# Two weight sums of attention's values formed in DRAM, a bias loaded around its masked corner, and squares ahead of low parts

## The chip, the core and the metric

One core of one Trainium2 chip runs the kernel. The metric is device time of one execution in microseconds (us). The kernel before takes 2188.28 us, the median of 3 runs (2187.18 to 2188.38). The execution that the profiler recorded is a further one and took 2192.47 us; the span from its first to its last instruction is 2190.8 us.

A core has one TensorE (PE; its weight loads are shown as PEld), one VectorE (DVE), one ScalarE (ACT), one GpSimd (POOL) and SyncE (SP), which here only issues transfers. 16 DMA engines carry the transfers of all queues. [...]

## What is computed

One layer of an encoder for 512 tokens of width 2048, all in 32-bit floats. `h = RMSNorm(x)` is multiplied by one input projection, whose columns give two head groups. Group A is attention with 16 heads of 64, over the own chunk of 64 tokens and the 8 chunks before it, with a learned bias by relative distance. Group B is gated linear attention with 4 heads. Both results go through `w_out` and are added to x. A gated MLP with a causal convolution of width 3 follows (two up-projections of 5632 columns, one down-projection), then a gate by a per-layer embedding, and a last RMSNorm.

```python
s = einsum('bqhd,bkhd->bhqk', qc, kb) * scale + bias      # attention, one chunk of queries
s = where(valid, s, neg); pr = softmax(s); y = einsum('bhqk,bkhd->bqhd', pr, vb)
x = x + concat(y_a, y_g) @ w_out
u = causal_depthwise_conv(rms_norm(x) @ w_ffn_up); x = x + (gelu(u_gate) * u_val) @ w_ffn_down
x = x + sigmoid(rms_norm(x) @ w_ple_gate) * (p @ w_ple_proj);  out = rms_norm(x)
```

With 512 tokens, 8 chunks of 64 and a band of 9 chunks, attention is causal by chunks: a query sees all keys of its own chunk and of those before it. Two chunks of queries share one tile of 128 rows, so in the last 128 keys of a tile the first 64 rows must not see the last 64 keys. That 64 x 64 corner is the masked corner of the bias tile.

## The kernel before

**Products with seven multiplications.** The large matrix products are done by a Strassen-like scheme: weights and activations are split into 2 x 2 blocks, and seven products P1, P2, P6, P5, P7, P3, P4 of block sums give the four blocks of the result (`PRODUCTS`). The weight operands are L11, L12, L22 (blocks as they are) and the sums S1 = L21+L22, S2 = S1+L11, S4 = S2+L12, S3 = L21+L11. Each 32-bit operand is further split in two parts, a high part (ACT copies the page to a reduced type) and a low part (DVE subtracts the high part from the page), and each product is three matmuls: high x high, high x low, low x high. So every weight page of 128 x 1024 costs one ACT copy, one DVE subtraction, and then matmuls on PE. The high/low pages of weights live in a ring of three.

**The stages in order.** (1) `first_values` and `second_values`: the values of group B, a plain product over 16 blocks of the contraction, in two halves of 512 columns; 8 weight pages each, with 24 matmuls of 512 columns a page. In the same time the root mean square of x, the gates and the pieces and block differences of the normed x are formed. (2) The values of attention by seven products (`VALUE_ORDER`: P1, P2, P4, P5, P6, P3, P7), four weight pages each, numbered n = 0 to 27, with 12 matmuls of 512 columns a page. (3) The front stage: 16 units of the input projection, each seven products of 24 matmuls of 256 columns. The first four units feed the linear attention, the next eight the attention (`attend`), the last four the output gates. (4) `wo`, the up-projection, three slices of the down-projection, the embedding gate, the end.

**Order of the work.** In the values' stages the order on ACT, DVE, PE, SP and POOL is the order in which the code is written (`in_order(True, True)`, L1423); in the later stages the loads may move. A wait of one instruction holds up all that stands behind it on its engine. `keep_in_program_order` puts one instruction behind what was written before it for its engine.

**The value pages of attention.** `values_product` (L1205) does for page n, in this order: load page n+4 if it is among the first 12, split page n+2 (`value_split`: ACT's high part, DVE's low part), do what the plan at L1581 lists for n, then PE's 12 matmuls. P1, P2 and P4 use L11, L12 and L22, loaded by SP into a ring of four pages. For S1, S2, S4, one page a block j stays in SBUF (`sum_load` L1182 loads L21 at n = 1, 3, 5, 7) and grows: for j = 0, 1 POOL accumulates L22 onto it (`sum_more` at n = 4 and 6), for j = 2, 3 DVE adds the L22 page, kept from P4 (`sum_right` L1192 at n = 10 and 11). After P5's split POOL accumulates L11 (n = 11 to 14, pages of P6), after P6's split L12 (n = 15 to 18, pages of P3). For P7, SP loads L21 into the ring at n = 7, 8, 11, 12, and POOL accumulates L11 at n = 8, 9, 19, 20.

**Attention's bias.** One tile of 128 x 2 x 512 holds the bias of the two heads of a unit. Unit 0's is loaded by `first_bias` (L1621), each later one by `load_e` (L813), 2 transfers of 256 KB, after the unit before has read the tile last. Then `mask` (L817) has DVE write the corner with -1e30, four steps after the unit's products, and two steps later `soft(0)` (L855) reads the bias first.

**A step.** In the front stage and later each step is one product of one unit: items of rank 0 (transfers), the high part of step i+2 (`prep_high`), items of rank 1, the low part of step i+2 (`prep_low`, L1646), the product, items of rank 2 to 8, the collection of the product.

**Squares.** In the stages `wo` and the last slice of the down-projection, `squares` (L627) adds the squares of the result to `acc`, ACT squaring and DVE adding; PE's sum over `acc` (tile `ms`) stands after the twelfth product of the next stage (`norm_step`, L1146), and its place on PE is fixed.

Of the kernel before, what the change touches and what calls it, by code (L numbers as in the profile page):

```python
# [12 lines left out]
ALU = mybir.AluOpType  # L13

P = 128
T = 512
# [26 lines left out]
def encoder_block(ctx: ExitStack, tc: tile.TileContext, A, out):  # L43
# [210 lines left out]
    def first_values(src, second):  # L254
        ps = [psum_mm(f"v0_{t}") for t in range(TT)]
        for kp in range(KD // 2):
            if kp == 4:
                gate_weights()
            xs = []
            if kp > 0:  # L260
                xs.append(load_input(2 * kp))
            hi, lo = wtile(src[0, kp], f"wv0_{kp}", 2 if kp < 2 else 1,
                           (lambda: xs.append(load_input(0))) if kp == 0 else None)
            xs.append(load_input(2 * kp + 1))
            sq_acc(xs[0], kp == 0)
            sq_acc(xs[1], False)
            if kp == KD // 2 - 1:
                in_order(True)
                first_stats()
            values_page(ps, hi, lo, kp)  # L270
        next(second)
        values_out(ps, 0, [gt(f"t{t}") for t in range(TT)])
# [354 lines left out]
    def squares(unit, at, c=slice(0, T)):  # L627

        def square(s):
            if unit.first and s == 0:  # L630
                act.activation(acc[:, c], unit.xs[:, s, c], AF.Square)
            else:
                sqt[unit, s] = tp.tile([P, T], F32, tag=("sq", "dg")[s], name="sq")[:, c]
                act.activation(sqt[unit, s], unit.xs[:, s, c], AF.Square)

        def add(s):
            if (unit, s) in sqt:
                vec.tensor_tensor(acc[:, c], acc[:, c], sqt[unit, s], ALU.add)

        return [(at + i, k, lambda f=f, s=s: f(s)) for i, k, f, s in ((0, 2, square, 0), (1, 2, square, 1), (1, 2, add, 0),  # L640
                                                                      (2, 2, add, 1))]

    sqt = {}

# [154 lines left out]
        move(3)  # L799


    TILES = ((3,), (2,), (1, 0))
    att, bias = [], []
    ypair = []

    def attend(unit):
# [4 lines left out]
            return att[0].tile([P, cols], dt, tag=tag or name, name=name, bufs=bufs)  # L811

        def load_e():  # L813
            for s in range(2):
                nc.sync.dma_start(bias[0][:, s, :], A["bias"][2 * b + s])

        def mask():  # L817
            vec.memset(bias[0][0:64, :, T - CHUNK:T], NEG)

        def load_v():  # L820
            M["V"] = tile_("va", T).rearrange("p (k v) -> p k v", k=TT)
# [364 lines left out]
    def sum_more(v, n, name):  # L1186
        prod, j = v["pages"][n]
        raw = v["raw"][n] if prod == "P7" else v["sum"][j]
        v["raw"][n] = raw
        pool.dma_start(raw, value_page(name, j), accum_op=ALU.add)  # L1190

    def sum_right(v, j):  # L1192
        vec.tensor_tensor(v["sum"][j], v["sum"][j], v["l22"].pop(j), ALU.add)
        v["raw"][12 + j] = v["sum"][j]

    def value_split(v, n):
        if n < len(v["pages"]):
            raw = v["raw"].pop(n)
            if v["pages"][n][0] == "P4":
                v["l22"][v["pages"][n][1]] = raw  # L1200
# [187 lines left out]
    def second_values(src):  # L1388
        raw, tiles = {}, {}
        first = {"ps": None}  # L1390

        def load(k):
            if k < KD // 2:
                raw[k] = page("wr", f"wv1_{k}_r")
                syn.dma_start(raw[k], src[1, k])
            else:
                if k == KD // 2:
                    use_rings({"wr": ("r1", "r2", "r0", "r3")})
                value_load(va, k - KD // 2)
# [9 lines left out]
        todo = {0: [(gate_low,), (scale_pair, 2), (right, 0)],  # L1409
                1: [(scale_pair, 3), (differences, 0), (right, 1)],  # L1410
                2: [(gate_up,), (gate_abs, (0, 1)), (scale_pair, 4), (gate_min, (0, 1))],
                3: [(gate_abs, (2, 3)), (scale_pair, 5), (gate_min, (2, 3)), (right, 2)],
                4: [(gate_exp, (0, 1, 2, 3)), (scale_pair, 6), (differences, 1), (right, 3)],
                5: [(gate_ln, (0, 1, 2, 3)), (scale_pair, 7), (differences, 2)],
                6: [(spread_differences, 0), (differences, 3), (spread_differences, 1)],
                7: [(spread_differences, 2), (spread_differences, 3), (right, 4), (differences, 4)]}
        for k in range(3):
            load(k)
        split_page(0)
        split_page(1)  # L1420
        load(3)
        yield
        in_order(True, True)  # L1423
        scale_pair(0)
        scale_pair(1)
        ps = [psum_mm(f"v1_{t}") for t in range(TT)]
        for k in range(KD // 2):
            load(k + 4)
            split_page(k + 2)
# [132 lines left out]
        nc.gpsimd.memset(G["attn"], 0.0)  # L1562
        G["s"] = pg.tile([P, 2, T], F32R, tag="r6", name="squares")

    va = dict(pages=[(p, j) for p in VALUE_ORDER for j in range(4)], raw={}, sum={}, l22={}, tiles={}, have=set())

    def at_page(n, *fs):
        plan.setdefault(n, []).extend(fs)
# [11 lines left out]

    for n, *fs in ((0, (second_out, (0, 1)), (spread_differences, 4)),  # L1581
                   (1, (second_out, (2, 3)), (sum_load, va, 0), (right, 5), (right, 6)), (2, (differences, 5)),
                   (3, (sum_load, va, 1), (spread_differences, 5)), (4, (right, 7), (sum_more, va, 12, "L22")),
                   (5, (sum_load, va, 2), (differences, 6)), (6, (sum_more, va, 13, "L22"), (spread_differences, 6)),
                   (7, (sum_load, va, 3), (differences, 7)), (9, (spread_differences, 7)),
                   (12, (gate_sum, (0, 1))), (13, (gate_scan, (0,))), (14, (gate_sum, (2, 3))), (15, (gate_scan, (1,))),
                   (16, (gate_scan, (2,))), (17, (gate_scan, (3,))),
                   (10, (sum_right, va, 2)), (11, (sum_right, va, 3)),
                   *((i, (value_load, va, 24 + j)) for j, i in enumerate((7, 8, 11, 12))),
                   *((11 + j, (sum_more, va, 16 + j, "L11")) for j in range(4)),  # L1590
                   *((15 + j, (sum_more, va, 20 + j, "L12")) for j in range(4)),
                   *((i, (sum_more, va, 24 + j, "L11")) for j, i in enumerate((8, 9, 19, 20))),
                   *((18 + i, (gate_decay, (i,))) for i in range(4)),
                   *((22 + i, (gate_small, (i,))) for i in range(4)), (26, (linear_pages,)),
                   *((n, (give, tag)) for n, tag in ((19, "r4"), (20, "r5"), (23, "r1"), (24, "r2"), (25, "r0"), (26, "r3")))):
        at_page(n, *(lambda f=f, a=a: f(*a) for f, *a in fs))
# [308 lines left out]
```

## Time and profile before

| what | us |
|---|---|
| median of 3 runs | 2188.28 |
| the profiled execution | 2192.47 |
| its span | 2190.8 |
| PE busy in the span | 2174.8 (99%) |
| DVE busy | 1862.3 (85%) |
| ACT busy | 1332.1 (61%) |
| POOL busy | 215.0 (10%) |

A row of the timeline gives the start, the duration of a run of like instructions, engine, line, operation, the tile written and the tiles read, shapes, their number, and in brackets the engine's idle time before it with what ended it. Most instructions carry line 64, a helper's, so they are told apart by tiles: `v` are the matmuls of group B's values, `vaA` to `vaD` those of attention's values (vaA first P1, then P6, then P7; vaB P2; vaD P4; vaC P5, then P3), `accA` to `accC` those of the later units, `w` the high and low parts of weights, `wva_s` the growing sum pages, `wva_P_r` the ring pages, `psc` scores, `sc` the scores with bias, `ptr` transposed probabilities, `ms` the sum of squares. PE's rows overlap a little, since matmuls are pipelined; the pace is read from starts. SPq and POOL rows of DMA_DIRECT2D are issues; the transfer itself lands later.

### The profile page before, as it was taken

The numbers are of one execution on the slowest core, as the hardware profiler recorded it, in microseconds if no ns is written. First come the engines' busy times: TensorE is split into PE (matmuls) and PEld (weight loads), VectorE is DVE, ScalarE is ACT, GpSimd is POOL, SyncE is SP. The second block draws the span as 40 slices with busy tenths as digits, with TensorE's granted clock in tenths as the row PEclk, the third lists the DMA queues.
The fourth block names the chain that finished last, engine by engine and source line by source line (L and its number), as shares of the span: only waits on it lengthen the run. The fifth ranks groups of instructions, "written<-read, shape, count | busy, mean of one in ns | idle before, by whom it ended". The sixth has DMA issues, their size and how long they took to land.

```text
span 2190.8 us, 45672 instructions
## 1 busy us (share of the span) xinstructions
PE 2174.8 (99%) x18262; PEld 2126.2 (97%) x18262; DVE 1862.3 (85%) x2558; ACT 1332.1 (61%) x1976; POOL 215.0 (10%) x261
## 2 busy tenths in 40 slices
PE   9999999999999999999999999999999999999998
PEld 7879998999999999999999999999999999999998
DVE  6977878887788889999888888888898787898898
ACT  6654567777675665555555555555564554666766
POOL 0121011111000011111111100000000101000000
PEclk9999999999999999999999999999999999999999
DMA  5598888898978989999999987887875976979996
GB/s 193 168 262 228 221 242 228 227 245 239 373 266 261 362 234 278 290 298 300 290 278 290 271 240 215 228 221 202 261 249 159 302 221 179 325 253 353 292 286 223
DMA packets 198277, 561.65 MB, mean 256 GB/s; under 512 B 21968, under 2 KB 60112, under 8 KB 198064
## 3 DMA queue, kind: packets, MB, share of 16 engines
q1 hardware_dynamic: 161824, 432.07, 55.3%
q0 software_dynamic: 34656, 124.27, 30.1%
q8 instruction: 143, 2.34, 0.4%
q10 hardware_dynamic: 1584, 2.40, 0.3%
q14 instruction: 70, 0.57, 0.1%
HBM read 485.25 MB, written 119.54 MB: 276 GB/s over the span
## 4 chain that ended last, share of the span: by engine, by line
PE 89%; DVE 4%; DMA 3%; ACT 2%; issue 1%; POOL 0%; DVEq 0%; POOLq 0%; ACTq 0%
PE accA L64 45%; PE accC L64 23%; PE accB L64 11%; PE v L64 4%; DMA s<-in_w_blk 1%; DVE w L64 1%; PE pp L64 1%; DMA wva_s<-in_w_v_a 1%; PE py L64 1%; PE ptr L64 1%; PE psc L64 1%; DMA bias<-in_bias 1%; ACT w L64 1%; PE po L64 1%; PE vaA L64 0%
## 5 line engine op out<-in xcount | busy, mean ns | idle before, releaser
L64 PE MATMUL accA<-h,w 128*128 128x256 f32 x5088 | 612.8, 277 | 0.0
L64 PEld LDWEIGHTS accA<-h,w 128*128 128x128 f32 x5088 | 594.6, 188 | 2.1 <-issue 0.9
L64 DVE TENSOR_TENSOR w<-s,w 128x1024 fp32r<-128x1024 f32 (+1 forms) x381 | 457.8, 1202 | 79.8 <-ACT w L64 79.3
L64 PE MATMUL accC<-h,w 128*128 128x256 f32 x4248 | 509.4, 277 | 0.0
L64 PEld LDWEIGHTS accC<-h,w 128*128 128x128 f32 x4248 | 494.4, 188 | 0.3
L64 ACT ACTIVATE w<-l 128x1024 fp32r<-128x1024 f32 (+1 forms) x320 | 332.4, 1039 | 173.8 <-PE accC L64 118.2
L64 DVE TENSOR_TENSOR w<-l,w 128x1024 fp32r<-128x1024 f32 (+1 forms) x320 | 383.3, 1198 | 62.9 <-ACT w L64 62.7
L64 ACT ACTIVATE w<-s 128x1024 fp32r<-128x1024 f32 (+1 forms) x381 | 394.9, 1037 | 29.7 <-DVE s L64 15.6
L64 ACT ACTIVATE u<-accA 128x256 f32<-128x256 f32 x302 | 114.3, 378 | 358.0 <-PE accA L64 355.5
L64 DVE TENSOR_TENSOR s<-s,l 128x1024 f32<-128x1024 f32 (+1 forms) x176 | 211.4, 1201 | 18.2 <-DMA s<-in_w_blk 12.7
L64 POOL DMA_DIRECT2D s<-in_w_up x84 | 73.9, 880 | 716.4 <-DMA s<-in_w_up 251.9
L64 DVE SCALAR_TENSOR_TENSOR cv<-u,cw,cv 128x511 f32<-128x511 f32 (+1 forms) x176 | 131.7, 748 | 3.1
L64 PE MATMUL accB<-up_R,w 128*128 128x256 f32 x1056 | 126.7, 276 | 0.0
L64 PE MATMUL accA<-up_N,w 128*128 128x256 f32 x1056 | 126.6, 276 | 0.0
L64 PE MATMUL accA<-up_R,w 128*128 128x256 f32 x1056 | 126.6, 276 | 0.0
L64 PEld LDWEIGHTS accB<-up_R,w 128*128 128x128 f32 x1056 | 123.0, 188 | 0.0
L64 PEld LDWEIGHTS accA<-up_N,w 128*128 128x128 f32 x1056 | 122.9, 188 | 0.0
L64 PEld LDWEIGHTS accA<-up_R,w 128*128 128x128 f32 x1056 | 122.9, 188 | 0.0
L64 ACT ACTIVATE u<-accC 128x256 f32<-128x256 f32 x98 | 37.5, 383 | 90.9 <-PE accC L64 90.6
L64 PE MATMUL v<-w,h 128*128 128x512 f32 x384 | 88.3, 391 | 0.1
L64 PEld LDWEIGHTS v<-w,h 128*128 128x128 f32 x384 | 72.0, 188 | 15.5 <-ACT g_t L64 0.5
L64 ACT ACTIVATE cv<-u,cw 128x512 f32<-128x512 f32 x88 | 67.1, 810 | 29.6 <-DVE u L64 29.6
(312 smaller groups left out, 2844.7 us busy)
## 6 DMA issues: line engine op xcount, KB each, us to landing
l<-in_w_up SPq DMA_DIRECT2D x132, 512.0 KB, 6.4
s<-in_w_up SPq DMA_DIRECT2D x84, 512.0 KB, 6.4
s<-in_w_up POOLq DMA_DIRECT2D x84, 512.0 KB, 7.7
l<-in_w_dn SPq DMA_DIRECT2D x56, 448.0 KB, 5.7
l<-in_w_blk SPq DMA_DIRECT2D x48, 512.0 KB, 6.1
s<-in_w_blk SPq DMA_DIRECT2D x32, 512.0 KB, 4.6
s<-in_w_blk POOLq DMA_DIRECT2D x32, 512.0 KB, 8.1
l<-in_w_out SPq DMA_DIRECT2D x28, 512.0 KB, 5.0
```

What stands on the lines that cost most here:

```text
L64: ins = f(*args, **kw)
```

## The change

It has three parts.

1. S1 and S3 of attention's value weights, four pages each, are made in DRAM. SP copies L21 from DRAM to a scratch page in DRAM (`value_sum_begin`), and POOL accumulates L22 (for S1) or L11 (for S3) onto it (`value_sum_add`). The four copies for S1 are put behind the last loads of `first_values`; the adds for S1, the copies for S3 and the adds for S3 are put into the pages k = 0 to 5 of `second_values`. `sum_load` and P7's `value_load` then load finished sums. `sum_right`, the two accumulates of L22 and the four of L11 for P7 go. The accumulates of L11 and L12 that turn S1 into S2 and S4 stay.
2. The corner of the bias tile is written once by DVE, in `first_bias`, ahead of the load. Each load of a unit's bias is 4 transfers in place of 2: rows 0 to 63 without the last 64 columns, rows 64 to 127 whole, for each of the two heads. `mask` goes.
3. In `squares`, the DVE adds of a stage's last two units have rank 1 in place of 2, so they come ahead of `prep_low` of their step and not behind it.

```diff
@@ first_values, last page
                 in_order(True)
+                for j in range(4):
+                    value_sum_begin("S1", j)
                 first_stats()
@@ squares
-        return [(at + i, k, lambda f=f, s=s: f(s)) for i, k, f, s in ((0, 2, square, 0), (1, 2, square, 1), (1, 2, add, 0),
-                                                                      (2, 2, add, 1))]
+        k = 2 if unit.last is None else 1
+        return [(at + i, j, lambda f=f, s=s: f(s)) for i, j, f, s in ((0, 2, square, 0), (1, 2, square, 1), (1, k, add, 0), (2, k, add, 1))]
@@ attend
+    def load_bias(h):
+        for s in range(2):
+            for r, n in ((slice(0, 64), T - CHUNK), (slice(64, P), T)):
+                nc.sync.dma_start(bias[0][r, s, :n], A["bias"][h + s, r, :n])
         def load_e():
-            for s in range(2):
-                nc.sync.dma_start(bias[0][:, s, :], A["bias"][2 * b + s])
-
-        def mask():
-            vec.memset(bias[0][0:64, :, T - CHUNK:T], NEG)
+            load_bias(2 * b)
...
-        items = [(2, 7, load_e if b else lambda: None), (2, 2, high), (3, 1, low), (4, 2, low_copy), (4, 1, mask), (5, 0, load_v), (11, 1, result)]
+        items = [(2, 7, load_e if b else lambda: None), (2, 2, high), (3, 1, low), (4, 2, low_copy), (5, 0, load_v), (11, 1, result)]
@@ values of attention
+    value_sums = {(s, j): scratch(f"wva_{s}{j}", (P, 1152))[:, :1024] for s in ("S1", "S3") for j in range(4)}
+    def value_sum_begin(s, j):
+        tc.keep_in_program_order(nc.sync.dma_start(value_sums[s, j], value_page("L21", j)))
+    def value_sum_add(s, j):
+        tc.keep_in_program_order(nc.gpsimd.dma_start(value_sums[s, j], value_page({"S1": "L22", "S3": "L11"}[s], j), accum_op=ALU.add))
     def value_load(v, n):
-        syn.dma_start(raw, value_page("L21" if prod == "P7" else PRODUCTS[prod][0], j))
+        syn.dma_start(raw, value_sums["S3", j] if prod == "P7" else value_page(PRODUCTS[prod][0], j))
     def sum_load(v, j):
-        syn.dma_start(raw, value_page("L21", j))
+        syn.dma_start(raw, value_sums["S1", j])
+        v["raw"][12 + j] = raw
-    def sum_right(v, j):
-        vec.tensor_tensor(v["sum"][j], v["sum"][j], v["l22"].pop(j), ALU.add)
-        v["raw"][12 + j] = v["sum"][j]
@@ second_values
+        sums = {0: [(add, "S1", 0), (add, "S1", 1), (begin, "S3", 0)], 1: [(add, "S1", 2), (add, "S1", 3), (begin, "S3", 1)],
+                2: [(begin, "S3", 2), (add, "S3", 0)], 3: [(begin, "S3", 3), (add, "S3", 1)], 4: [(add, "S3", 2)],
+                5: [(add, "S3", 3)]}
@@ second_values, page k, ahead of its matmuls
+            for f, *a in sums.get(k, ()):
+                f(*a)
@@ the plan of the value pages
-                   (3, (sum_load, va, 1), (spread_differences, 5)), (4, (right, 7), (sum_more, va, 12, "L22")),
-                   (5, (sum_load, va, 2), (differences, 6)), (6, (sum_more, va, 13, "L22"), (spread_differences, 6)),
+                   (3, (sum_load, va, 1), (spread_differences, 5)), (4, (right, 7)),
+                   (5, (sum_load, va, 2), (differences, 6)), (6, (spread_differences, 6)),
-                   (10, (sum_right, va, 2)), (11, (sum_right, va, 3)),
-                   *((i, (sum_more, va, 24 + j, "L11")) for j, i in enumerate((8, 9, 19, 20))),
@@ first_bias
-        for s in range(2):
-            nc.sync.dma_start(bias[0][:, s, :], A["bias"][s])
+        vec.memset(bias[0][0:64, :, T - CHUNK:T], NEG)
+        load_bias(0)
```

More of the change, by code (lines that the diff above doesn't have):

```diff
@@ L1179, in value_load @@
         raw = v["raw"][n] = page("wr", f"wva_{prod}{j}_r")
-        syn.dma_start(raw, value_page("L21" if prod == "P7" else PRODUCTS[prod][0], j))
+        syn.dma_start(raw, value_sums["S3", j] if prod == "P7" else value_page(PRODUCTS[prod][0], j))
     def sum_load(v, j):
         raw = v["sum"][j] = pg.tile([P, 1024], F32, tag=SUM_TAGS[j], name=f"wva_s{j}")
-        syn.dma_start(raw, value_page("L21", j))
+        syn.dma_start(raw, value_sums["S1", j])
+        v["raw"][12 + j] = raw
     def sum_more(v, n, name):
-        prod, j = v["pages"][n]
-        raw = v["raw"][n] if prod == "P7" else v["sum"][j]
-        v["raw"][n] = raw
+        raw = v["raw"][n] = v["sum"][v["pages"][n][1]]
+        j = v["pages"][n][1]
         pool.dma_start(raw, value_page(name, j), accum_op=ALU.add)
-    def sum_right(v, j):
-        vec.tensor_tensor(v["sum"][j], v["sum"][j], v["l22"].pop(j), ALU.add)
-        v["raw"][12 + j] = v["sum"][j]
     def value_split(v, n):
@@ L1198, in value_split @@
             raw = v["raw"].pop(n)
-            if v["pages"][n][0] == "P4":
-                v["l22"][v["pages"][n][1]] = raw
             hi, lo = v["tiles"][n] = weight_pages(72 if n < 26 else 24)
@@ L1416, in second_values @@
                 7: [(spread_differences, 2), (spread_differences, 3), (right, 4), (differences, 4)]}
+        begin, add = value_sum_begin, value_sum_add
+        sums = {0: [(add, "S1", 0), (add, "S1", 1), (begin, "S3", 0)], 1: [(add, "S1", 2), (add, "S1", 3), (begin, "S3", 1)],
+                2: [(begin, "S3", 2), (add, "S3", 0)], 3: [(begin, "S3", 3), (add, "S3", 1)], 4: [(add, "S3", 2)],
+                5: [(add, "S3", 3)]}
         for k in range(3):
@@ L1563, in linear_pages @@
         G["s"] = pg.tile([P, 2, T], F32R, tag="r6", name="squares")
-    va = dict(pages=[(p, j) for p in VALUE_ORDER for j in range(4)], raw={}, sum={}, l22={}, tiles={}, have=set())
+    va = dict(pages=[(p, j) for p in VALUE_ORDER for j in range(4)], raw={}, sum={}, tiles={}, have=set())
     def at_page(n, *fs):
```

## The prediction

> **What bounds the kernel now.** I read the page first, then the waits of PE, then PE's timeline around each wait, and last the chain of waits and the DMA queues there. The page, then PE's own waits (engine, tile, whom it waited for: us in total, times, longest):
>
> ```profile
> span 2190.8 us, 45672 instructions
> PE 2174.8 (99%) x18262; PEld 2126.2 (97%) x18262; DVE 1862.3 (85%) x2558; ACT 1332.1 (61%) x1976; POOL 215.0 (10%) x261
> ```
> ```profile
> PE ptr L64 <- DVE sc L64: 2.0, 2, 1.3
> PE accB L64 <- DVE w L64: 1.4, 2, 0.8
> PE ms L64 <- DVE acc L64: 0.9, 2, 0.7
> ```
>
> PE sets the end: it is idle for 16 us of 2190.8, part of it the start and the tail. The change takes no matmul away, so all it can win are these few waits. Each is somewhat longer than shown, since the idle time counts only from the modelled end of pipelined matmuls; I take the loss from starts.
>
> **Part 1, the sums of the value weights.** PE's timeline of attention's values (48 matmuls are one product):
>
> ```profile
> 121.21 11.04 PE L64 MATMUL vaD<-w,h 128*128 128x512 f32 x48
> 132.09 11.04 PE L64 MATMUL vaC<-w,h 128*128 128x512 f32 x48
> 143.77 0.49 PE L64 MATMUL vaA<-w,h 128*128 128x512 f32 x1 [0.64 <-ACT w L64]
> 155.81 6.00 PE L64 MATMUL vaC<-w,in_R 128*128 128x512 f32 x25
> 167.31 11.12 PE L64 MATMUL vaA<-w,h 128*128 128x512 f32 x48
> 178.26 2.90 PE L64 MATMUL accA<-in_R,w 128*128 128x256 f32 x24
> ```
>
> An undisturbed product takes 132.09 - 121.21 = 10.88 us. P5 takes 11.68, P6 12.04, P3 11.50 and P7 10.95, so 46.17 - 43.52 = 2.65 us are lost. What is late is P6's first page, S1 + L11. The chain, ACT's row for that page, POOL's issues ahead of it, and the queues' loads from 110 to 160 us (packets, MB, share of 16 engines):
>
> ```profile
> 129.52 13.03 DMA wva_s<-in_w_v_a
> 145.27 7.33 DMA wva_s<-in_w_v_a
> ```
> ```profile
> 142.66 1.06 ACT L64 ACTIVATE w<-wva_s 128x1024 fp32r<-128x1024 f32 x1 [6.54 <-DMA wva_s<-in_w_v_a]
> ```
> ```profile
> 127.35 0.92 POOL L64 DMA_DIRECT2D wva_P_r<-in_w_v_a  x1 [2.02 <-ACT h L64]
> 128.71 0.91 POOL L64 DMA_DIRECT2D wva_P_r<-in_w_v_a  x1 [0.43 <-issue]
> ```
> ```profile
> q0 software_dynamic: 2023, 7.31, 72.9%
> q1 hardware_dynamic: 1586, 5.77, 30.1%
> ```
>
> Here q0 (POOL) needs 0.729 x 50 us / 7.31 MB = 5.0 us a MB, so one accumulate of a 0.524 MB page occupies the engines for 2.6 us; a plain load (q1) for 1.4 us. The accumulate issued at 129.52 lands 13.03 us later. Two others, for P7, stand just ahead of it, and the change removes both: 13.03 - 2 x 2.6 = 7.8 us, near the 7.33 of the later row. It may take 11.1 us without harm: P5 would end at 132.09 + 10.88 = 142.97, and the split ahead of P6 takes 1.06 (ACT) and at most 1.24 (DVE's low part of such a page, as the row of part 3 has it). So the wait goes, with 3 us in hand. The next three adds follow at PE's pace and keep it. Bounds for this gain: 0 (still late) to 2.65; I take **2.5**, as the row at 145.27 is nearest. Removing two DVE adds and four more accumulates only widens the margin.
>
> What is late next is the first units of the front stage:
>
> ```profile
> 200.14 1.23 DVE L64 TENSOR_TENSOR s<-s,l 128x1024 f32<-128x1024 f32 x1 [4.92 <-DMA s<-in_w_blk]
> 202.55 1.21 PE L64 MATMUL accB<-in_R,w 128*128 128x256 f32 x8 [0.53 <-DVE w L64]
> ```
>
> This too ends with an accumulate. Its load waits for a page that DVE frees, so it starts earlier as PE does, and two of the removed accumulates (P7's last) stood shortly ahead of this stage's first sums. I take **+0.3**. Bounds: +0.7, the stall with its tail, if it goes; -2.5, if this accumulate keeps its clock time and takes back all that was won.
>
> **What the moved sums cost.** Eight copies from DRAM to DRAM and eight accumulates there come earlier; the stretches 25 to 54 and 54 to 103 us (busy time by engine, clock, DMA share, GB/s), an SP load of that time, the ACT instruction that reads it, and the landing times of the sums that the kernel already makes in DRAM:
>
> ```profile
> 25.00:54.00 29.00, 29.00 (x154) 22.17 (x153) 15.91 (x26) 14.73 (x22) 0.85 (x3) 1.00 0.29 89
> 54.00:103.00 49.00, 48.91 (x216) 40.18 (x215) 44.69 (x70) 33.58 (x50) 4.25 (x6) 1.00 0.46 151
> ```
> ```profile
> 71.03 0.33 SPq L64 DMA_DIRECT2D wv_r<-in_w_v_g  x1
> ```
> ```profile
> 83.33 1.07 ACT L64 ACTIVATE w<-wv_r 128x1024 fp32r<-128x1024 f32 x1
> ```
> ```profile
> DMA to landing us min/median/max: 5.1/10.8/15.2
> ```
>
> S1's copies (4 x 1.4 = 6 us of engine time, 10 if a copy costs as much as an accumulate) fall into a stretch with 0.71 x 29 = 20 us free. S3's copies and the eight adds (4 x 1.4 + 8 x 2.6 = 26 us, at most 31) fall into one with 0.54 x 49 = 26 us free. So the engines become full there, and loads become slower, but each of these pages is asked for 12.3 us ahead of its split (83.33 - 71.03), and even 10.8, the median landing of such sums, is under that. POOL has nothing else to issue; SP waits for nothing before a copy. I take **0**; if the cover is gone, rival C gives the price.
>
> **Part 2, the bias.** DVE and PE at the second attention unit, and two rows of the chain, the bias and an undisturbed run of matmuls:
>
> ```profile
> 356.57 0.17 DVE L64 MEMSET bias<- 64x128 f32 x1 [5.29 <-DMA bias<-in_bias]
> 359.70 0.68 DVE L64 CUSTOM_DVE_ANT_0 sc<-psc,bias 128x512 f32<-128x512 f32 x1
> 363.29 0.49 DVE L64 TENSOR_SCALAR sc<-sc,mx 128x512 f32<-128x512 f32 x1
> ```
> ```profile
> 355.10 1.98 PE L64 MATMUL accB<-in_R,w 128*128 128x256 f32 x16
> 357.91 1.19 PE L64 MATMUL accB<-in_R,w 128*128 128x256 f32 x8 [0.82 <-DVE w L64]
> 359.62 2.89 PE L64 MATMUL accA<-h,w 128*128 128x256 f32 x24
> 363.83 1.25 PE L64 MATMUL ptr<-ident,sc 128*128 128x128 f32 x8 [1.32 <-DVE sc L64]
> ```
> ```profile
> 342.33 14.11 DMA bias<-in_bias
> 1591.69 10.88 PE accA L64 x96
> ```
>
> DVE stands 5.29 us before the memset, with two low parts of weights and the scores queued behind it. PE's pace is 10.88 / 96 = 0.1133 us a matmul of 256 columns (24 in 2.72), so accB goes on at 357.91 where 356.91 was due, and ptr starts at 363.83 where 362.34 was due: 1.00 + 1.49 = 2.49 us. Without the memset DVE goes on at 356.57 - 5.29 = 351.28, and the 1.00 is gone. The first to want the bias is then the score. Its second head waits for the transfer that lands at 342.33 + 14.11 = 356.44; with two more issues by SP I allow 0.7 and say 357.1, against 359.70 before. Then all behind it comes 2.6 us earlier, the normed scores at 363.78 - 2.6 = 361.2, and PE wants them at 361.34. That is just in time: I take **2.2**. Bounds: 2.49, and 1.0 if the pieces land 1.5 us later than I allow; 0 if they land 2.5 us later still. The other seven memsets (0.17 each) cost PE nothing; the new one in `first_bias` neither, as DVE is idle between its instructions there and the scores come 30 us later.
>
> [...]
>
> **Part 3, the squares.** Around the last slice of the down-projection:
>
> ```profile
> 2046.05 5.60 PE L64 MATMUL accC<-h,w 128*128 128x256 f32 x48
> 2052.32 1.05 PE L64 MATMUL ms<-ones,acc 128*128 128x1 f32 x8 [0.68 <-DVE acc L64]
> ```
> ```profile
> 2050.43 1.24 DVE L64 TENSOR_TENSOR w<-l,w 128x1024 fp32r<-128x1024 f32 x1
> 2051.56 0.70 DVE L64 TENSOR_TENSOR acc<-acc,sq 128x512 f32<-128x512 f32 x1
> ```
>
> PE is free at 2046.05 + 48 x 0.1133 = 2051.49 and starts ms at 2052.32: 0.83 lost. With the add first, `acc` is done by 2051.1. The low part comes 0.6 us later, but its matmuls are the last third of the product behind ms. At the other place, near 789 us, it is the rest of the waits' row, 0.9 - 0.7 = 0.2, and with the pipelined tail some 0.35. I take **1.15**, bounds 0 to 1.2.
>
> **The sum.** 2.5 + 0.3 + 2.2 + 1.15 = 6.15 us. The profiled execution goes from 2192.47 (span 2190.8 and 1.7 around it) to 2186.3. The median of the runs shown is 4.2 lower than that execution; with the same distance it goes from 2188.28 to **2182.1**.
>
> **Rivals.** *A, the gain of the values is given back.* The accumulate before 200.14 keeps its clock time, and PE waits there for what it won: 6.15 - 0.3 - 2.5 = 3.35, so 2184.9. For it: DVE waits 4.92 us there, the longest wait in this argument but one. Against: its issue hangs on pages that PE's progress frees.
>
> *B, the bias is the next wait.* The four pieces land 1.5 us or more later than I allow, and PE waits at ptr as before: 6.15 - 1.2 = 4.95, so 2183.3. For it: 14.11 us to land in a full queue, and only 0.15 us in hand. [...]
>
> *C, the sums in DRAM are too slow, and SP stands at P7's loads.* Nothing in SP's order can pass those four loads, and the front's first weights stand behind them; their median landing from 110 to 160 us, and the split of the first:
>
> ```profile
> l<-in_w_blk SPq DMA_DIRECT2D x2, 512.0 KB, 9.1
> ```
> ```profile
> 172.95 1.06 ACT L64 ACTIVATE w<-l 128x1024 fp32r<-128x1024 f32 x1 [1.66 <-PE vaA L64]
> ```
>
> If the eight adds go one after another from 54 us on, c each, the last sum is there at 54 + 8c and the front's weights at 63 + 8c, wanted by 172.95 - 2.5 = 170.4. That costs from c = 13.4 on and eats the whole gain at 14.2. At 15.2, the longest landing of such sums, they come at 184.7, 14.3 late: 2188.3 + 14.3 - 6.15 = 2196.4, slower. Against it: one add occupies the engines for 2.6, not 15.
>
> *D, nothing moves*, since the adds behind P5 stay late and DVE, 85% busy, finds other waits: only part 3 and the 1.00 of part 2 are left, 2.15 in all, so 2186.1.
>
> **How the numbers follow.** Forecast 0.55, A 0.14, B 0.15, C 0.06, D 0.10. About 0.2%, 4.4 us, is what a measurement of this kernel tells from no change. Faster by more than that: the forecast, and most of B, 0.64 with what misses of single terms take off; within it: A, D and the rest, 0.29; slower: C and what I don't see, 0.07. The range: below, all upper bounds together give 2.65 + 0.7 + 2.49 + 1.2 = 7.0, so 2181.2, and a distance between runs of about 1 us makes it 2180.3; above it reaches over B and A to D: 2186.5. C is left out.
>
> **What the profile after would show.** Part 1: P5 to P7 take 10.9 us each, ACT has no wait for wva_s before 143 us, and DMA share in 54 to 103 us is near 1; wrong, if ACT still waits there, or if loads before 100 us hold ACT up. Front: accB near 200 us waits 0.5 us or less. Part 2: no memset in the loop, accB without a wait, ptr with none or little; wrong, if DVE waits for the bias in front of the score by several us. Part 3: ms starts with no wait. The forecast falls if PE's idle time is not some 6 us lower, whatever the single waits do.

## The result, and the profile after

The changed kernel takes 2185.23 us (median of 22 runs, 2182.42 to 2188.45) against 2188.33 us of the kernel before on the same chip (22 runs, 2184.47 to 2192.52). The ratio is 0.9986, with a 95% interval of 0.9980 to 0.9993: 3.1 us faster, between 1.5 and 4.4. That lies within the range predicted, 3.1 us above the forecast of 2182.1, and is 0.14%, not the more than 0.2% that I had held likeliest.

The median lies 0.3 us from the number of rival A (2184.9) and far from the forecast, so only the traces can tell which mechanism was at work. The profiled execution of after took 2185.19 us, 7.3 less than that of before (2192.47). So the two traces differ by more than twice what the times do, and this is what the experiments had to clear up. First the page of after, then PE's waits (engine, tile, whom it waited for: us in total, times, longest):

```profile
span 2183.3 us, 45706 instructions
PE 2172.0 (99%) x18262; PEld 2125.9 (97%) x18262; DVE 1860.2 (85%) x2549; ACT 1333.2 (61%) x1976; POOL 216.3 (10%) x263
```
```profile
PE pw L88 <- POOL ones L82: 1.2, 1, 1.2
PE accA L64 <- ACT u L64: 0.8, 1, 0.8
PE ptr L64 <- DVE sc L64: 0.7, 1, 0.7
PE ms L64 <- DVE q L64: 0.3, 1, 0.3
```

The rows accB and ms <- acc of the prediction are gone, one of the two waits of ptr too, and so are the values' waits (vaA and vaC in the waits of before); one row, accA <- u, is new. PE's timeline of after at the places of the prediction (attention's values, the front's accB, the second attention unit, the last ms, the new wait):

```profile
132.78 11.04 PE L64 MATMUL vaC<-w,h 128*128 128x512 f32 x48
143.66 11.04 PE L64 MATMUL vaA<-w,h 128*128 128x512 f32 x48
...
176.37 2.90 PE L64 MATMUL accA<-in_R,w 128*128 128x256 f32 x24
...
198.15 2.88 PE L64 MATMUL accB<-in_R,w 128*128 128x256 f32 x24
200.87 2.89 PE L64 MATMUL accA<-h,w 128*128 128x256 f32 x24
...
351.73 2.89 PE L64 MATMUL accB<-in_R,w 128*128 128x256 f32 x24
355.15 2.89 PE L64 MATMUL accA<-h,w 128*128 128x256 f32 x24
357.88 1.03 PE L64 MATMUL ptr<-ident,sc 128*128 128x128 f32 x8
359.68 2.88 PE L64 MATMUL accC<-h,w 128*128 128x256 f32 x24
...
1174.13 2.99 PE L64 MATMUL accB<-up_R,w 128*128 128x256 f32 x24
1177.88 3.01 PE L64 MATMUL accA<-up_N,w 128*128 128x256 f32 x24 [0.77 <-ACT u L64]
...
2040.51 5.61 PE L64 MATMUL accC<-h,w 128*128 128x256 f32 x48
2045.95 0.95 PE L64 MATMUL ms<-ones,acc 128*128 128x1 f32 x8
```

The rows in the first four groups and the last one run without a gap, so they give the undisturbed distance of two starts: 176.37 - 132.78 = 43.59 us from P5 to the front, 2.72 from accB to accA, 359.68 - 351.73 = 7.95 from accB over ptr to accC, 5.44 from accC to ms. Whatever another trace has above these is PE's loss there. In the first trace of before these losses are 2.58, 0.84, 11.03 - 7.95 = 3.08, and 0.83 + 0.36 at the two ms: 7.7 us. The spans differ by 2190.8 - 2183.3 = 7.5 us. That is not these four places alone: after loses 1.03 us at the new wait (1177.88 - 1174.13 - 2.72), and smaller differences elsewhere make up for it.

The prediction had named one sign more: PE's idle time some 6 us lower. It reads 16.0 us before and 11.3 after, 4.7 lower. The same 18262 matmuls also show 2.8 us less busy time (2174.8 and 2172.0), so part of what was waited stood in the busy time.

The price of the moved sums is seen in the stretches 25 to 54 and 54 to 103 us (as in the prediction: busy time by engine, clock, DMA share, GB/s), and in the issues of 110 to 160 us:

```profile
25.00:54.00 29.00, 29.00 (x154) 22.16 (x153) 15.28 (x25) 14.05 (x21) 3.34 (x5) 1.00 0.55 176
54.00:103.00 49.00, 48.91 (x216) 40.19 (x215) 45.22 (x70) 33.59 (x50) 7.76 (x10) 1.00 0.93 270
```
```profile
wva_s<-in_w_v_a POOLq DMA_DIRECT2D x8, 512.0 KB, 5.6
```

The DMA share doubles from 0.46 to 0.93 between 54 and 103 us, PE's busy time there stays at 48.91, and the eight adds of 110 to 160 us land in 5.6 us (median), where the first add behind P5 took 13.03.

### The profile page after: what moved, and what is told of

It is laid out like the page before. It is cut to its first block, busy times and chain, and to the rows that moved or that the text cites. A ratio compares the mean times of both kernels' runs of the same rounds, so it can differ in the third digit from the quotient of the medians.

```text
span 2183.3 us, 45706 instructions
## 1 busy us (share of the span) xinstructions
PE 2172.0 (99%) x18262; PEld 2125.9 (97%) x18262; DVE 1860.2 (85%) x2549; ACT 1333.2 (61%) x1976; POOL 216.3 (10%) x263
## 4 chain that ended last, share of the span: by engine, by line
PE 94%; DMA 3%; DVE 1%; ACT 1%; issue 1%; DVEq 0%; SPq 0%; ACTq 0%; POOL 0%; POOLq 0%
PE accA L64 46%; PE accC L64 23%; PE accB L64 12%; PE v L64 4%; PE vaA L64 1%; DMA s<-in_w_up 1%; PE pp L64 1%; PE vaC L64 1%; PE py L64 1%; PE psc L64 1%; PE ptr L64 1%; DMA l<-in_w_up 1%; PE po L64 1%; PE vaD L64 0%; PE vaB L64 0%
```

## The experiments

Theories ahead of the first four runs: *S*, the sum of 6.15 holds; *V*, the waits are real, but their size changes from execution to execution and the first trace was unlucky; *G*, the gain is given back at a later wait. All ratios are to the kernel before on the same chip.

**The kernel before, twice more.** No edit.

> The kernel before, once more, for a second execution with a trace. Theory S (the sum holds: the waits of the first trace are the usual ones): P5 to P7 of the values take some 46.2 us again (2.6 over 43.5), accB near 202 us waits 0.7, accB and ptr near 357 us lose 2.5, the two starts of ms 1.2. Theory V (the waits that end with a transfer change from execution to execution, and the first trace, 4.2 us over the median, had long ones): ms loses 1.2 again, as no transfer stands behind it, but the values lose 1.5 or less, or the bias arrives sooner than 14.1 us after its issue and accB and ptr lose 1.5 or less; the span is 2 to 4 us shorter than 2190.8.

> The kernel before, unchanged, for a further trace. Theory V (the size of its waits follows how long single transfers take in that execution): the accumulate for P6's first page lands 11 to 13 us after its issue, and PE's loss in P6 and P3 is 0.6 us at 11.5 and 2.2 us at 13.0; DVE's wait for the bias near 352 us lies between 1.7 and 5.3 us, and PE's loss at accB and ptr behind it follows it, none at 1.7, 1.1 to 1.4 us at 3.7 to 4.0, 2.5 us at 5.3; ms waits 0.36 and 0.8 to 1.0 us in any case. Theory S (the first trace showed the usual sizes): 2.2 us or more in the values and 2.5 us behind the bias again. Ratio 1 within its interval.

Ratios 0.9998 (0.9989 to 1.0007) and 1.0004 (0.9995 to 1.0013), as they must be. Their traces differ from the first. ACT's first high part of P6 and DVE at the bias, in the second trace and then in the third:

```profile
140.69 1.06 ACT L64 ACTIVATE w<-wva_s 128x1024 fp32r<-128x1024 f32 x1 [4.69 <-DMA wva_s<-in_w_v_a]
...
351.11 0.17 DVE L64 MEMSET bias<- 64x128 f32 x1 [1.66 <-DMA bias<-in_bias]
```
```profile
142.61 1.06 ACT L64 ACTIVATE w<-wva_s 128x1024 fp32r<-128x1024 f32 x1 [5.96 <-DMA wva_s<-in_w_v_a]
...
354.47 0.17 DVE L64 MEMSET bias<- 64x128 f32 x1 [4.09 <-DMA bias<-in_bias]
```

ACT waited 6.54 us in the first trace, here 4.69 and 5.96; DVE 5.29, here 1.66 and 4.09. PE's rows of the second trace, at the same places as above:

```profile
131.97 11.04 PE L64 MATMUL vaC<-w,h 128*128 128x512 f32 x48
...
176.94 2.90 PE L64 MATMUL accA<-in_R,w 128*128 128x256 f32 x24
...
353.17 2.89 PE L64 MATMUL accB<-in_R,w 128*128 128x256 f32 x24
...
361.11 2.88 PE L64 MATMUL accC<-h,w 128*128 128x256 f32 x24
...
2042.25 5.60 PE L64 MATMUL accC<-h,w 128*128 128x256 f32 x48
2048.66 1.05 PE L64 MATMUL ms<-ones,acc 128*128 128x1 f32 x8 [0.80 <-DVE acc L64]
```

The values lose 44.97 - 43.59 = 1.38 us, the bias nothing (7.94), ms 0.97. V holds: what waits for a transfer varies (the bias cost 3.08 us in the first trace and nothing here), what waits for DVE's order hardly does (this start of ms 0.83 and 0.97).

**Each part alone.** The edit of each is that part of the diff above, put into the kernel before.

> Part 1 alone: the sums S1 and S3 of the value weights made in DRAM, the rest as before. Theory S: 2.8 us faster, the values' P5 to P7 in 43.6 us and no wait of accB near 200 us. Theory V: 0.5 to 1.8 us faster. Theory G (the waits go, but work that comes earlier waits later): the values in 43.6 us, and the same time taken back after 200 us, so within 0.5 us of before.

> Part 2 alone: the corner of the bias written once, each load in four pieces around it. Theory S: 2.2 us faster, accB near 357 us without a wait and ptr with none or little. Theory V: 0.5 to 1.5 us faster. [...]

> Part 3 alone: the adds of the last two units' squares ahead of the low parts. All theories: both starts of ms (near 789 and 2052 us) without a wait, 1.15 us faster; theory G: the low parts that come 0.6 us later make PE wait in the product behind ms, and nothing is won.

Ratios: sums 0.9993 (0.9984 to 1.0002), bias 0.9997 (0.9989 to 1.0006), squares 0.9997 (0.9988 to 1.0006). No single part can be told from nothing by its time. Multiplied they give 0.9987, close to the 0.9986 of the whole change, but the interval of each is wider than its gain. The traces tell them apart: in the values, at the bias and at ms each part removes its own wait and leaves the others. DVE at the bias in the kernel with the sums alone, which keeps the memset:

```profile
351.62 0.17 DVE L64 MEMSET bias<- 64x128 f32 x1 [3.73 <-DMA bias<-in_bias]
```

PE's losses in us by the distances of starts, in all traces that have the code of before at a place, and in the two of the changed kernel ("-": that part is in):

| trace | values | accB, 200 us | bias | two ms |
|---|---|---|---|---|
| before, first | 2.58 | 0.84 | 3.08 | 1.19 |
| before, second | 1.38 | 0.63 | 0 | 1.34 |
| before, third | 2.00 | 0 | 1.99 | 1.17 |
| squares alone | 1.30 | 0 | 1.84 | - 0 |
| bias alone | 1.94 | 0 | - 0 | 1.32 |
| sums alone | - 0 | - 0 | 1.62 | 1.17 |
| changed, first and second | - 0 | - 0 | - 0 | - 0 |
| mean with the code of before | 1.84 | 0.29 | 1.71 | 1.24 |

At the bias the loss is DVE's wait less a slack: 5.29, 4.09, 3.95 (squares alone), 3.73 and 1.66 us of wait cost PE 3.08, 1.99, 1.84, 1.62 and 0, so the slack is some 2.1 us. The means add up to 5.1 us. Of accB near 200 us the table shows less than of the others: three of the five traces without part 1 lose nothing there either, so that part 1 removes this wait is likely and not shown.

The last column is the distance to the start of ms alone. Behind the last ms part 3 takes a little back. The 48 matmuls of accA there take 5.73 or 5.74 us in place of 5.53 or 5.54 (2046.77 to 2052.50 in the trace of after, 2053.24 to 2058.77 in the first of before), in every trace with part 3 and in none without it, and the 8 of ms take 0.82 in place of 0.92. Counted from accC to the product behind those 48, part 3 gains 0.71 to 0.86 us at this place and not 0.82 to 0.97.

**The changed kernel once more.** No edit.

> The changed kernel once more, nothing altered, for a second trace and more times. Theory V (each step does what it says, but the first trace of the kernel before had longer transfer waits than usual): about 3 us faster than the kernel before, ratio 0.998 to 0.9993 again; in the trace P5 to P7 at 10.9 us each with no wait for wva_s before 143 us, no wait of accB near 200 and 357 us, no wait of ms at either place; the waits that this change does not touch (ptr near 333 us, accA for u near 1178 us) stay at 0.3 to 1.4 us. Theory L (the changed kernel was the lucky one, its waits come back in other executions): waits over 0.5 us at P6 or P3 or at ptr near 360 us, and a ratio over 0.9993.

Ratio 0.9986 again (0.9977 to 0.9995). P5 to the front takes 43.59 us, accB to accC 7.95, accC to ms 5.44: all four gains recur, V holds, not L. But its profiled execution (2187.18 us) is 2.0 slower than the first, and one place costs more than that. PE's rows there and the stretches around them:

```profile
1172.41 1.98 PE L64 MATMUL accB<-up_R,w 128*128 128x256 f32 x16
1174.65 1.20 PE L64 MATMUL accB<-up_R,w 128*128 128x256 f32 x8 [0.26 <-DVE w L64]
1177.60 4.63 PE L64 MATMUL accA<-up_N,w 128*128 128x256 f32 x24 [1.76 <-ACT u L64]
1182.07 2.89 PE L64 MATMUL accC<-h,w 128*128 128x256 f32 x24
```
```profile
1175.00:1177.60 2.60, 0.84 (x8) 0.64 (x6) 2.56 (x4) 1.84 (x4) 1.31 (x2) 1.00 0.77 255
1177.60:1180.00 2.40, 2.40 (x15) 2.40 (x16) 2.18 (x3) 2.38 (x3) 1.05 (x2) 0.71 0.92 157
1180.00:1182.00 2.00, 2.00 (x11) 2.00 (x11) 1.97 (x4) 0.00 (x0) 0.31 (x1) 0.50 1.08 185
```

accB to accA takes 5.19 us in place of 2.72, and the next 24 matmuls 4.47 in place of 2.72, at a granted clock of 0.71 and 0.50. This is the wait that was new in the page of after. Its chain: DVE waits for an accumulated page of the up-projection, adds a bias to `u` behind it, ACT's convolution waits for that, and ACT's copy of accA, which PE wants, stands behind the convolution. DVE's wait in the first trace of before, the first of after and this one, in that order:

```profile
1176.80 1.23 DVE L64 TENSOR_TENSOR s<-s,l 128x1024 f32<-128x1024 f32 x1 [1.37 <-DMA s<-in_w_up]
```
```profile
1172.51 1.23 DVE L64 TENSOR_TENSOR s<-s,l 128x1024 f32<-128x1024 f32 x1 [3.42 <-DMA s<-in_w_up]
```
```profile
1172.23 1.23 DVE L64 TENSOR_TENSOR s<-s,l 128x1024 f32<-128x1024 f32 x1 [4.64 <-DMA s<-in_w_up]
```

Again the loss is the wait less a slack of some 2.2 us: 1.37 costs 0, 2.79 (before, second) 0.63, 2.98 (sums alone) 0.82, 3.42 costs 1.03, 4.64 costs 2.47. It occurs in the kernel before too (0.63 in its second trace) and with the bias alone (1.43), so the change doesn't make it. Whether the change makes it longer is open: the six traces without the whole change lose 0.54 on average there, the six with it (four of them variants below, those with doubled traffic left aside) 1.19 with the clock's share. But two of these six lose nothing, and one alone, this one, gives 4.22.

**The sums without the early traffic.** The eight copies and eight adds are left out, and S1's and S3's loads read L21 itself. So S1 lacks L22 and S3 lacks L11, and the kernel computes other values of attention; its matmuls and loads into SBUF are the same in number:

```diff
-                for j in range(4):
-                    value_sum_begin("S1", j)
-            for f, *a in sums.get(k, ()):
-                f(*a)
-        syn.dma_start(raw, value_sums["S3", j] if prod == "P7" else value_page(PRODUCTS[prod][0], j))
+        syn.dma_start(raw, value_page("L21" if prod == "P7" else PRODUCTS[prod][0], j))
-        syn.dma_start(raw, value_sums["S1", j])
+        syn.dma_start(raw, value_page("L21", j))
```

> The changed kernel without the eight copies and eight adds in DRAM; the loads of the sum pages and of P7's pages read L21 itself. So S1 lacks L22 and S3 lacks L11, and attention's values are not the reference's; matmuls and loads are the same in number. Theory N (the early traffic costs nothing): same time as the changed kernel, ratio to before 0.998 to 0.9993, DMA share of 54 to 103 us back at about 0.46, loads of that time landing in 3 to 5 us in place of 9 to 12, and PE's start of P1 at the same time within 0.3 us. Theory T (the full engines cost PE something before 126 us): P1 starts earlier by over 0.5 us, and the ratio is lower than the changed kernel's by as much.

Ratio 0.9987 (0.9978 to 0.9996), that of the changed kernel within the interval. Its stretch of 54 to 103 us:

```profile
54.00:103.00 49.00, 48.91 (x216) 40.18 (x215) 45.05 (x70) 33.59 (x49) 3.99 (x6) 1.00 0.47 150
```

The share falls to 0.47 and PE's busy time doesn't move. P1 to P7 run without a gap in both. The early traffic, 0.46 x 49 + 0.27 x 29 = 30 us of engine time, costs PE nothing as it stands.

**The early traffic doubled, whole and in part.** A copy and an add onto a spare page beside each of the eight (first kernel), or beside the four of S1 (second):

```diff
+    spare_sums = {(s, j): scratch(f"wvb_{s}{j}", (P, 1152))[:, :1024] for s in ("S1", "S3") for j in range(4)}
     def value_sum_begin(s, j):
+        tc.keep_in_program_order(nc.sync.dma_start(spare_sums[s, j], value_page("L21", j)))
     def value_sum_add(s, j):
+        tc.keep_in_program_order(nc.gpsimd.dma_start(spare_sums[s, j], value_page({"S1": "L22", "S3": "L11"}[s], j), accum_op=ALU.add))
```

> The changed kernel with each early copy and each early add done a second time, onto spare pages that nobody reads: 26 us more of engine time (8 x 1.4 and 8 x 2.6, less for what falls before 54 us), where the changed kernel has 0.07 x 49 = 3.4 us free from 54 to 103 us. If rival C was far off: the last S3 add lands before 120 us in place of 91.5, P7's loads (issued from about 130 us) do not wait, the loads of 54 to 103 us land in 12 to 20 us, and PE loses 0 to 3 us there, so ratio 0.998 to 1.0005. If rival C was near: SP stands at P7's loads or ACT waits for group B's value pages by over 5 us in all, and the kernel is slower than before by 2 us or more.

> The changed kernel with the four S1 copies and adds alone done a second time, onto spare pages that nobody reads: 5.6 us more of engine time before 54 us, 10.4 us more after it. With all eight done twice the kernel lost 21 us against the changed one. Theory F (the engines are the bound: what does not fit into the 3.4 us free from 54 to 103 us is lost whole): PE loses 10.4 - 3.4 = 7 us, at group B's last pages or at P1's first ones, ratio to before about 1.002. Theory M (the loads' lead of 12 us covers a burst of this size): no wait of PE before 126 us, the loads of 54 to 82 us land in up to 20 us, ratio 0.998 to 0.9993 as the changed kernel.

All eight twice: ratio 1.0083 (1.0069 to 1.0096), 18 us slower than before and 21 slower than the changed kernel. S1's four twice: 1.0020 (1.0011 to 1.0029), 7.4 us slower than the changed kernel, where theory F gave 7. But of the places that F named the trace shows 3.0, in P1 (113.45 - 99.54 - 10.88), and 0.4 more in P2 (124.76 - 113.45 - 10.88). The rest isn't located, so F's number is met and its mechanism is shown in part. The landing times of group B's pages from 55 to 110 us (min/median/max) in the changed kernel and in the two, and PE's rows of the first:

```profile
DMA to landing us min/median/max: 9.3/10.5/12.0
```
```profile
DMA to landing us min/median/max: 16.6/22.0/28.5
```
```profile
DMA to landing us min/median/max: 9.7/12.3/16.0
```
```profile
100.41 0.80 PE L64 MATMUL v<-w,h 128*128 128x512 f32 x1 [4.78 <-ACT w L64]
101.67 8.02 PE L64 MATMUL v<-w,h 128*128 128x512 f32 x23 [0.47 <-DVE w L64]
```

The pages are asked for 12.3 us ahead. At up to 12.0 us nothing is lost; at up to 16 group B still gets through, but P1's own pages then land after up to 19.4 us in place of 10.7 (window 60 to 125 us), and P1 loses 3.0; at up to 28.5 PE loses some 19 us until P2 starts (130.50 in place of 111.02). So the change stands inside its cover, but not far from its end. The share of the engines reads 1.05 (S1's twice) and 1.04 (all twice) from 54 to 103 us, so a share of 1 is not quite the ceiling, and the room that the changed kernel leaves is between 0.07 x 49 = 3.4 and 0.12 x 49 = 5.9 us.

**The bias in whole rows.**

```diff
-            for r, n in ((slice(0, 64), T - CHUNK), (slice(64, P), T)):
-                nc.sync.dma_start(bias[0][r, s, :n], A["bias"][h + s, r, :n])
+            for r, c in ((slice(0, P), slice(0, T - CHUNK)), (slice(64, P), slice(T - CHUNK, T))):
+                nc.sync.dma_start(bias[0][r, s, c], A["bias"][h + s, r, c])
```

> The changed kernel with the bias loaded as one transfer of 128 rows by 448 columns and one of 64 rows by 64 columns for each head, in place of 64 rows by 448 and 64 rows by 512. Bytes and number of transfers are the same. [...] Either way PE does not wait for it except perhaps at ptr near 360 us, and the ratio is that of the changed kernel, 0.998 to 0.9993.

Ratio 0.9988 (0.9979 to 0.9997). Landing times of the bias in a quiet unit (404 to 418 us): the changed kernel, whole rows, and the 256 KB transfers of before:

```profile
DMA to landing us min/median/max: 2.3/2.5/2.6
```
```profile
DMA to landing us min/median/max: 2.5/2.6/3.0
```
```profile
DMA to landing us min/median/max: 3.1/3.2/3.3
```

A piece of half the rows (112 to 128 KB) holds half the bytes, so equal times a piece don't say which form is sooner; the whole bias does. From the first issue to the last landing the two heads take 4.4 us in half rows (issued from 409.0 to 410.8), 4.2 in whole rows (410.3 to 411.9) and 4.0 in the two whole tiles of before (415.6 and 416.5). No form lands a microsecond sooner than another. Larger pieces of half rows were not run.

In the full queues of the second unit the whole rows landed up to 13.7 us after their issue in this one execution, the half rows up to 10.7. There the score had to wait. The last piece landed at 354.2, DVE's second score began just behind it, and PE lost 0.57 us up to accC (360.79 - 352.27 - 7.95):

```profile
354.35 0.69 DVE L64 CUSTOM_DVE_ANT_0 sc<-psc,bias 128x512 f32<-128x512 f32 x1 [1.46 <-PE accB L64]
```

The wait is put down to accB, which came last of what the profile sees; that the piece ended it is read from the times.

**A further wait, that of ptr near 333 us.** By starts, PE waits 0.8 to 1.0 us there in all traces so far, for scores that DVE norms behind a low part. Two kernels norm them ahead of it, for one head and for both; the second in full:

```diff
-                (5, 6, scores), (6, 1, soft), (7, 1, normal), (7, 5, turn), (8, 1, evict), (8 + (h == 1), 4, values))]
+                (5, 6, scores), (6, 1, soft), (7 - (b == h == 0), 1, normal), (7, 5, turn), (8, 1, evict), (8 + (h == 1), 4, values))]
```

> The changed kernel, where in attention's unit 0 the scores of the first head are normed one step earlier, ahead of the low part of a weight page that DVE did first (1.23 us); nothing else differs. All traces but this one have PE wait 0.9 to 1.0 us for these scores at ptr near 333 us. If the order on DVE is the cause: that wait is 0.2 us or less, and PE comes 0.7 to 0.9 us earlier to the next product; nothing new over 0.3 us in the next two steps. If ACT's exponential or the bias is the cause, the wait stays at 0.9. By times it cannot be told from the changed kernel: ratio 0.9975 to 0.9993 either way.

> The changed kernel, where in attention's unit 0 the scores of both heads are normed ahead of the low part of the weight page, not the first head's alone. With the first head alone PE's wait at ptr moved from the first head (0.9 us) to the second (1.1 us, since its norm then stood behind the low part), and nothing was won. If the low part's place on DVE is the cause: the first head's transposes start without a wait, the second head's wait for ACT's exponential alone, 0.2 to 0.5 us, the low part comes 1 us later and delays nothing, and PE is 0.5 to 0.7 us earlier behind them. If the page's low part is needed that early: a new wait of accA or accC for w of 0.5 us or more within the next two products, and the gain is gone. Ratio 0.9970 to 0.9993; 0.6 us cannot be told by times.

Ratios 0.9977 (0.9967 to 0.9986) and 0.9982 (0.9973 to 0.9991): neither can be told from the changed kernel. PE in the first and in the second:

```profile
334.34 0.66 PE L64 MATMUL ptr<-ident,sc 128*128 128x128 f32 x4 [1.07 <-DVE sc L64]
```
```profile
332.17 0.66 PE L64 MATMUL ptr<-ident,sc 128*128 128x128 f32 x4 [0.18 <-DVE sc L64]
333.78 0.39 PE L64 MATMUL psc<-Kh,Q 128*128 128x256 f32 x1 [0.95 <-DVE mx L64]
```

The wait moves to the second head, and from there to the next scores, for which PE waits on DVE's `mx`. From the scores before it to the product behind it, PE takes 6.62 us in the changed kernel (328.90 to 335.52), 6.86 and 7.05 in these two. My expectation missed both times: a new order on DVE moves the wait and doesn't shorten the stretch. That DVE's work bounds it is how I read this; no run with less work on DVE shows it.

## Why the prediction was right, and where it was off

**Mechanisms.** The main steps did what they said. The waits in the values, at the bias and at ms are at nothing in both traces of the changed kernel, and back where their part is left out (at the bias in four of five traces). accB near 200 us is at nothing too, but so it is in three traces without part 1. The accumulate behind P5 lands in 5.6 us (I said 7.3 to 7.8); DVE no longer stands at a memset; ms starts at once; the moved sums cost nothing, by the run without them and not only by the count of 20 and 26 us free. One step was not quite free: the low part behind the squares, which I let come later at no price, goes with 0.2 us more in the product behind ms.

**The sum, 6.15, and the step to 2182.1.** The time lies in the range, but 3.1 us from the forecast, and the gain is half of the one predicted. The sum was off twice, in opposite directions. For its own execution the sum was too small: 7.7 us were lost there. Part 2 is most of that: 1.00 + 1.49 count the late starts of accB and ptr, but not the 0.5 us between ptr and accC, so 3.08 lay above the bound of 2.49; and accB near 200 us gave 0.84, above its bound of 0.7 and not 0.3. The larger error was the other one: I saw that the execution lay 4.2 us over the median and carried the distance over unchanged ("with the same distance it goes from 2188.28 to 2182.1"). The distance was partly made of these same waits. Over five traces each, parts 1 and 2 are worth 1.84 + 0.29 and 1.71, not 2.8 and 2.2; part 3, a matter of order, is worth 1.24 (I took 1.15). Together 5.1. The times say 3.1 (1.5 to 4.4). Two things lie between them, and neither is shown to be the cause. The traces with the change lose 0.65 more near 1178 us on average, most of it in one trace. And the profiled executions behind the 5.1 are still slower than usual: the six without the whole change took 2190.1 us on average, where the medians of the same six sets of runs average 2188.3; the six with it took 2185.7 against 2185.5. So the traces without the whole change lie 1.8 - 0.2 = 1.6 us further over the usual execution than those with it, as the first trace did by more. An estimate of 5.1 - 0.65 - 1.6 = 2.9 is near what the times say, but which waits are shorter in the usual execution no run here shows.

That 2185.2 lies inside the range is in part luck. The range was drawn upwards to take in rivals A, B and D, and none of them is what happened; no bound in it stood for a trace that oversizes its own waits.

**Chances.** Faster by over 0.2% needed 4.4 us; with a sum from one trace, 4.2 us over the median, 0.64 was too much, and the case between forecast and nothing should have had the larger share.

**Rivals.** A, the front's accumulate keeps its clock time: no, accB near 200 us runs without a gap, though A's number, 2184.9, is the nearest to what was measured. Something of its kind may stand near 1178 us, far from where I looked. B, the bias as the next wait: not in the changed kernel; the score waited for its matmul, not for the bias:

```profile
351.46 0.69 DVE L64 CUSTOM_DVE_ANT_0 sc<-psc,bias 128x512 f32<-128x512 f32 x1 [0.71 <-PE psc L64]
```

But B was near: the second score began at 352.35, 1.1 us behind the landing of the last piece (issued at 340.5, landed 10.7 us later), and with the bias in whole rows it did wait. My 357.1 for the last piece was too late by 5.9 us: 3.4 from the landing, which took 10.7 in place of the 14.11 that I had started from, and 2.5 from the issue, which came earlier because PE and all behind it did (accB starts at 351.73 in place of 355.10). D: no, its waits went. C is real, but in another place and from another point on than I worked out: not SP at P7's loads from 13.4 us an add, but group B's and P1's pages, once the engines have more to do than the 3.4 to 5.9 us left free. The queues share the engines: with POOL's adds and SP's copies doubled, SP's loads landed after up to 28.5 us in place of 12.0.

## What to carry to other kernels

A wait that a transfer ends cost its lateness less a slack, at the bias (2.1 us) and near 1178 us (2.2 us). So one trace that lies over the median can show it too long: take such a wait from several traces, and carry a trace's sum to the median only after asking which waits make up the distance. The wait that an order of instructions made, ms, recurred in every trace (1.17 to 1.34) and could be taken at its size. Where idle DMA time pays for a change, state how much is left: here 3.4 to 5.9 us, and an estimated 10.4 us more (four adds of 2.6) cost 7.

## What the runs showed of the hardware that I had not expected

Some waits of PE cost twice. After 1.76 us idle near 1177 us the granted clock, 1.00 until 1177.6, was 0.71 to 1180 and 0.50 to 1182, and 24 matmuls took 4.47 us in place of 2.72; after 4.78 us, with all sums doubled, it was 0.50 from 100.4 to 105 us and 0.79 from 105 to 110, and 23 matmuls took 8.02 in place of the 5.53 of those from 90.10 on. Other waits left it at 1.00: 2.71 us in P1 with S1's sums doubled, 1.62 near 1180 us in the same kernel, 1.27 there with the bias alone. So the length of a wait alone doesn't set it; what does, no run here shows.

The four issues of a bias in pieces take SP 0.48 to 0.59 us each, the two of before 0.33. In the kernel of after, of before and with whole rows, 404 to 418 us (duration in ns, min/median/max):

```profile
L807 SPq DMA_DIRECT2D bias<-in_bias x4: 475/567/589, 409.0 to 410.8; - x4
```
```profile
L815 SPq DMA_DIRECT2D bias<-in_bias x2: 328/330/332, 415.6 to 416.5; - x2
```
```profile
L807 SPq DMA_DIRECT2D bias<-in_bias x4: 333/474/536, 410.3 to 411.9; - x4
```

The number of rows alone doesn't set it: with whole rows the two issues of 128 rows took 0.33 (the first) and 0.54 us, those of 64 rows 0.47 and 0.48. Whether it is the shape or that four issues follow each other closely was not tried.
